# Attention's output projection as seven block products, four more weight blocks split by VectorE, and a longer lead for DMAs

## The chip, the cores and the metric

The kernel runs on one core of one Trainium2 chip. The metric is device time in microseconds (us), the median of several executions. Engines are named as the profile names them: PE (TensorE, matmuls), DVE (VectorE), ACT (ScalarE), POOL (GpSimd), SP (SyncE, which here only issues transfers). A transfer is a DMA. The profile lists one execution.

## The reference

Two layers of a streaming encoder on 512 tokens of width 1024, in float32. Layer 0 is a convolution module and an MLP, layer 1 is latent attention and an MLP; each part is normed before and after and added to the stream h.

```python
# layer 0, convolution module
u = h @ w_pw1 + b_pw1
a, gate = jnp.split(u, 2, axis=-1)
u = a * jax.nn.sigmoid(gate)
u = lax.conv_general_dilated(u, ...)  # 31 taps, one filter for each channel
u = jax.nn.silu(layer_norm(u, ln_g, ln_b))
return u @ w_pw2 + b_pw2
# MLP of both layers
return jnp.square(jax.nn.relu(h @ w1)) @ w2
# layer 1, attention: o holds the 8 heads' outputs, 512 x 1024
return o @ w_o
```

## The kernel before

**Precision.** Each float32 matrix is kept as two parts, hi (the value rounded to the matmul's format) and lo (what that leaves out). A product is three matmuls: hi x hi, hi x lo, lo x hi. A weight block is 128 x 1024, read by SP into `raw` (5 buffers); ACT's copy makes `wh` (5 buffers), and DVE's subtraction `wl` (6 buffers). `weight` does this, in the order of the table `USE`. For blocks chosen by `lo_by_dma` the lower part is made in another way: ACT writes -hi into `wl`, and POOL issues a transfer that reads the block from DRAM a second time and adds it to `wl` (an accumulating transfer). In the first pointwise product this holds for the blocks from the fifth on (`i >= 4`).

**Convolution module.** `w_pw1` is 16 blocks, taken in pairs (a and gate of 128 channels): "block 0" to "block 7" below are these pairs. After a pair, DVE scales both by the norm, ACT takes the sigmoid, DVE makes u. In blocks 0, 1 and 3 the 31 taps are run by DVE and ACT. In blocks 2, 4, 5, 6 and 7 they are run by PE with Toeplitz matrices (read from `cw` by SP, nine transfers for a block), and u goes to DRAM and back to be dealt out over the partitions: one transfer `dealt<-big` and four `uu<-dealt`, all issued by ACT (`deal_tokens`, then `taps_tensor`). The taps of block 2 stand on PE behind the pair of block 4. The vector table `vt` holds the biases that the sigmoid needs.

**MLP.** The second product is done by Strassen's scheme: the 2 x 2 blocks of each side (halves of tokens by halves of the inner dimension, halves of the inner dimension by halves of the columns) give seven products instead of eight. Sides that are sums or differences are made first: on the left by DVE, on the right by a POOL transfer that adds the second block to `raw` (sum) or by a second read and a DVE subtraction (difference). The results are added to or taken from the output blocks by DVE.

**Attention's output projection.** `wo` runs `by_tokens`: for the first half of the columns all four token blocks together, then for the second half one token block after the other. 8 weight blocks, 192 matmuls of 128 x 512. `post_norm` takes each finished block: ACT's square into `junk` (a sum for the norm), DVE's product with the gain (`big<-big,row`), and when a pair of token blocks (0 and 1, or 2 and 3) is complete, its norm (small `stat` operations) and four additions to h (`h<-big,stat,h`). Then `prenorm`: PE transposes h into `bc` (eight 128-blocks by two token blocks), ACT and DVE write hi and lo of the next input, and FF1 of layer 1 begins on it, on 256 tokens at a time at first. This passage is called the joint below.

**What sets the order.** The code above records operations; the planner (`schedule`) orders them by estimated costs, and the engines' instructions come out in that order, all with the line of `issue` (L640). Each engine runs its list in order. A transfer isn't issued more than `LEAD` (16000 ns) ahead of its due time. Where the planner expects PE to wait long for a new accumulator, it puts identity matmuls there (`mm<-ident`, `bc<-ident` without a second source).

Of the kernel before, what the change touches and what calls it, by code (L numbers as in the profile page):

```python
# [11 lines left out]
ALU = mybir.AluOpType  # L12
# [68 lines left out]
PRODUCTS = ((3, 6, 2, 1, 4, 5, 7),) * 2 + ((3, 1, 4, 5, 7), (3, 5, 1, 4, 7))  # L81


BLK = {}
USE = []
_cols, _names = [], []
# [27 lines left out]
def _out(*name):  # L114

    for dh in range(2):
        for ku in range(4):
            _blk(name + (dh, ku))
# [24 lines left out]
_blk(("kr",))  # L143
for _m in range(3):
    _blk(("dq", _m))
for _u in range(-1, 16):
    for _key in PROJECTIONS.get(_u, ()):
        _blk(_key, {"uv": 512, "uqr": 384, "uq": 384, "uk": 256}[_key[0]])
_out("wo")
_ff(1)  # L150
NBLK = len(_cols)

# [95 lines left out]

PORT = ("tensor_tensor", "scalar_tensor_tensor")

LEAD = 16000.0

BESIDE = 3000.0

# [389 lines left out]
def trunk(ctx: ExitStack, tc: tile.TileContext, xT, xN, wts, vec, along, rope, cw, out):  # L644
# [28 lines left out]
    def pair():  # L673
        return big(F32R), big(F32R)

    def tmp():
        return nc.tile(TMP)
# [53 lines left out]
    def weight(key):  # L731

        while key not in blocks:
            name, parts = USE[len(blocks)]
            i, n = BLK[parts[0][0]], _cols[BLK[parts[0][0]]]
            if name[0] in GAINS:
                blocks[name] = scaled(name, wts[i])
                continue
            raw, hi, lo = nc.tile(RAW), nc.tile(WH, F32R), nc.tile(WL, F32R)
            step = 256 if i < 2 else n  # L740
            for o in range(0, n, step):
                nc.sync.dma_start(out=raw[:, o : o + step], in_=wts[i, :, o : o + step])
            for other, sign in parts[1:]:
                if sign > 0:
                    nc.gpsimd.dma_start(out=raw, in_=wts[BLK[other]], accum_op=ALU.add)
                else:
                    second = nc.tile(RAW)
                    nc.sync.dma_start(out=second, in_=wts[BLK[other]])
                    for o in range(0, n, 512):
                        nc.vector.tensor_tensor(  # L750
                            out=raw[:, o : o + 512], in0=raw[:, o : o + 512], in1=second[:, o : o + 512], op=ALU.subtract
                        )
            src = raw if len(parts) > 1 else wts[i]
            if i >= 4 and lo_by_dma(name):
# [203 lines left out]
        return y  # L958


    def feed_forward(layer, X, F):


# [4 lines left out]
        for q in range(4):  # L968
# [5 lines left out]
            for m, (t0, n) in order:  # L974
# [4 lines left out]
                for th, (a, w) in enumerate((HA, HB)):  # L979
                    if t0 <= a < t0 + n:  # L980
# [4 lines left out]
            def terms(p):  # L985

                left, A = STRASSEN[p][0], []
                for u in range(2):
                    src = Z[left[0][0]][u]
                    if len(left) > 1:  # L990
                        d = tmp()
                        nc.vector.tensor_tensor(out=d, in0=src, in1=Z[left[1][0]][u], op=ALU.subtract)
                        src = d
                    A.append(pair())
                    split(src, slice(0, T), A[u])
                return A

            def sides(q, p):
                return [weight(("ff2", layer, q, p, u)) for u in range(2)]

            def product(pts, A, w, steps, first=True, last=True):

                for u, i in steps:
                    if i not in pts:
                        pts[i] = nc.tile(MM)
                    hi, lo = w[u]
                    for j in range(2):
                        cs, ts = slice(j * DH, (j + 1) * DH), slice(j * 2 * P + i * P, j * 2 * P + (i + 1) * P)
                        for k, (a, c) in enumerate(((A[u][0], hi), (A[u][0], lo), (A[u][1], hi))):
                            nc.tensor.matmul(  # L1010
                                pts[i], lhsT=a[:, ts], rhs=c[:, cs],
                                start=(first and u == 0 and j == 0 and k == 0), stop=(last and u == 1 and j == 1 and k == 2),
                            )
                return pts

            def collect(p, pts):
                for i, pt in pts.items():
# [12 lines left out]
                F[b][to[1]] = acc[quad[to]][i]  # L1030
                return b, to[1]

            steps = [(u, i) for u in range(2) for i in range(2)]
            for p in PRODUCTS[q]:
                A = terms(p)
                collect(p, product({}, A, sides(q, p), steps))
                if q == 3 and p in (5, 7):
                    for i in range(2):
                        yield done((0, int(p == 5)), i)
            if q > 1:  # L1040
                for p in TOGETHER:
                    both[q, p] = terms(p)
            if q == 3:

                pts = {p: product({}, both[2, p], sides(2, p), steps, last=False) for p in TOGETHER}
# [241 lines left out]
    def token_blocks():  # L1287
        return [[big() for _ in range(2)] for _ in range(TB)]

    def mixer_out(layer, gen):  # L1290

        MF, r2 = token_blocks(), one(f"r2_{layer}", [P, TB])
# [148 lines left out]

    for b in range(TB):
        nc.sync.dma_start(out=h[b], in_=order[b * P : (b + 1) * P])
    O = [pair() for _ in range(KT)]
    ALL = slice(0, T)
    V, QR, KN, QN, PN = {}, {}, {}, {}, {}

# [89 lines left out]

    def project(u):
        for kind, n in PROJECTIONS.get(u, ()):
            {"uqr": rotary, "uv": values, "uk": keys, "uq": queries}[kind](n)  # L1540

    project(-1)
# [16 lines left out]
    Xn, r2 = mixer_out(1, wo)  # L1559
    F = [[None, None] for _ in range(TB)]  # L1560

    def finish(bs, rho):
# [133 lines left out]
```

## Time and profile before

| | us |
|---|---|
| median of 3 runs | 1066.44 (1065.2 to 1067.63) |
| the profiled execution | 1068.46 |
| its span | 1066.7 |
| TensorE busy | 1045.5 (98%) |
| VectorE busy | 764.1 (72%) |
| ScalarE busy | 640.9 (60%) |

The mean granted TensorE clock of the profiled execution is 0.993 of full speed. In lines of the profile, `out<-in` names the tiles, `xN` counts instructions, and what stands in brackets at an end is the idle time before the instruction and what ended it. Busy times of neighbours on PE overlap, so a matmul's price is read from the distance of starts, or from a full window by its count. In windows the columns are length, busy time and count for each engine, granted clock, share of time that the 16 DMA engines were busy, and GB/s.

### The profile page before, as it was taken

The numbers are of one execution on the slowest core, as the hardware profiler recorded it, in microseconds if no ns is written. First come the engines' busy times: TensorE is split into PE (matmuls) and PEld (weight loads), VectorE is DVE, ScalarE is ACT, GpSimd is POOL, SyncE is SP. The second block draws the span as 40 slices with busy tenths as digits, with TensorE's granted clock in tenths as the row PEclk, the third lists the DMA queues.
The fourth block names the chain that finished last, engine by engine and source line by source line (L and its number), as shares of the span: only waits on it lengthen the run. The fifth ranks groups of instructions, "written<-read, shape, count | busy, mean of one in ns | idle before, by whom it ended". The sixth has DMA issues, their size and how long they took to land. (4 is left out here: it accounts for less than half of the span.)

```text
span 1066.7 us, 15181 instructions
## 1 busy us (share of the span) xinstructions
PE 1045.5 (98%) x5284; PEld 884.7 (83%) x5284; DVE 764.1 (72%) x1559; ACT 640.9 (60%) x1343; POOL 141.6 (13%) x165
## 2 busy tenths in 40 slices
PE   8989999999999999999999999999999999999996
PEld 7878988988888888888888888889888888888885
DVE  6497994857438737959988987547574495497698
ACT  8543497766545446545767877558565554454652
POOL 1110011100100100001104533301010010000010
PEclk9989999999999999999999999999999999999998
DMA  9995888657866848658923132557599388485684
GB/s 288 300 254 171 287 211 236 156 168 207 253 171 190 257 126 241 189 182 227 237 69 93 56 100 81 174 182 179 161 245 253 112 235 257 143 243 168 187 237 129
DMA packets 67613, 204.08 MB, mean 191 GB/s; under 512 B 7632, under 2 KB 13904, under 8 KB 67536
## 3 DMA queue, kind: packets, MB, share of 16 engines
q1 hardware_dynamic: 49680, 150.15, 40.9%
q0 software_dynamic: 13536, 49.29, 25.6%
q10 hardware_dynamic: 4320, 3.68, 1.1%
q8 instruction: 41, 0.67, 0.3%
q14 instruction: 36, 0.29, 0.1%
HBM read 197.58 MB, written 5.51 MB: 190 GB/s over the span
## 5 line engine op out<-in xcount | busy, mean ns | idle before, releaser
L640 PE MATMUL mm<-big,wh 128*128 128x512 f32 (+1 forms) x1512 | 441.1, 374 | 1.2 <-ACT wh L640 1.2
L640 PE MATMUL mm<-wh,big 128*128 128x512 f32 (+1 forms) x1216 | 374.7, 387 | 0.0
L640 ACT ACTIVATE wh<-raw 128x512 fp32r<-128x512 f32 (+2 forms) x444 | 251.0, 612 | 117.7 <-PE mm L640 73.8
L640 PEld LDWEIGHTS mm<-big,wh 128*128 128x128 f32 x1512 | 275.6, 188 | 52.4 <-ACT wh L640 1.5
L640 DVE TENSOR_TENSOR wl<-raw,wh 128x512 fp32r<-128x512 f32 (+1 forms) x356 | 227.7, 680 | 106.5 <-ACT wh L640 104.1
L640 PE MATMUL mm<-big,wl 128*128 128x512 f32 (+1 forms) x756 | 282.5, 374 | 0.0
L640 PEld LDWEIGHTS mm<-wh,big 128*128 128x128 f32 x1216 | 226.3, 188 | 46.9
L640 PE MATMUL mm<-wl,big 128*128 128x512 f32 (+1 forms) x608 | 234.9, 387 | 0.1
L640 PEld LDWEIGHTS mm<-big,wl 128*128 128x128 f32 x756 | 142.6, 189 | 25.7 <-DVE wl L640 0.5
L640 PEld LDWEIGHTS mm<-wl,big 128*128 128x128 f32 x608 | 114.2, 188 | 23.4 <-DVE wl L640 0.2
L640 POOL DMA_DIRECT2D raw<-wts x64 | 55.5, 867 | 572.7 <-DMA raw<-wts 190.4
L640 ACT ACTIVATE big<-tmp 128x256 f32<-128x256 f32 (+1 forms) x208 | 95.9, 493 | 43.2 <-DVE tmp L640 37.3
L640 DVE TENSOR_TENSOR big<-big,big 128x512 f32<-128x512 f32 (+4 forms) x103 | 69.8, 698 | 55.9 <-ACT big L640 55.6
L640 ACT ACTIVATE tmp<-mm 128x512 f32<-128x512 f32 (+1 forms) x75 | 41.7, 556 | 103.1 <-PE mm L640 102.0
L640 PE MATMUL mm<-big,big 128*128 128x256 f32 (+3 forms) x520 | 83.5, 310 | 1.8 <-DVE big L640 1.8
L640 PEld LDWEIGHTS mm<-big,big 128*128 128x128 f32 x520 | 73.1, 189 | 7.0 <-DVE big L640 2.3
L640 ACT ACTIVATE big<-mm 128x512 f32<-128x512 f32 (+5 forms) x106 | 56.6, 537 | 33.9 <-PE mm L640 32.9
L640 DVE TENSOR_TENSOR big<-tmp,big 128x512 fp32r<-128x512 f32 (+1 forms) x96 | 60.9, 642 | 15.3 <-ACT big L640 12.7
L640 DVE SCALAR_TENSOR_TENSOR big<-big,vt,big 128x512 fp32r<-128x512 f32 (+29 forms) x95 | 63.3, 736 | 8.0 <-ACT big L640 8.0
L640 DVE TENSOR_TENSOR big<-big,mm 128x512 f32<-128x512 f32 x96 | 63.7, 683 | 3.2 <-PE mm L640 2.8
L640 DVE TENSOR_TENSOR tmp<-big,big 128x512 f32<-128x512 f32 x80 | 53.3, 686 | 8.9 <-ACT big L640 8.9
L640 POOL DMA_DIRECT2D wl<-wts x30 | 26.1, 869 | 213.0 <-ACT wl L640 113.3
(90 smaller groups left out, 775.9 us busy)
## 6 DMA issues: line engine op xcount, KB each, us to landing
raw<-wts SPq DMA_DIRECT2D x222, 512.0 KB, 5.0
raw<-wts POOLq DMA_DIRECT2D x64, 512.0 KB, 7.9
wl<-wts POOLq DMA_DIRECT2D x30, 512.0 KB, 8.4
big<-cw SPq DMA_DIRECT2D x45, 256.0 KB, 5.6
big<-wts SPq DMA_DIRECT2D x12, 256.0 KB, 4.3
row<-along SPq DMA_DIRECT2D x5, 512.0 KB, 5.5
raw<-wts SPq DMA_DIRECT2D x12, 192.0 KB, 2.7
big<-xT SPq DMA_DIRECT2D x8, 256.0 KB, 4.2
```

Of the source, the lines that this page charges most:

```text
L640: return f(*args, **kwargs)
```

## The change

Three things change.

1. The output projection is done by the Strassen scheme that the MLP has. Attention's outputs go into eight blocks `Z` (two ACT copies of 256 columns for each head) in place of the eight pairs `O`; `terms` makes the left sides, `product` runs 24 matmuls of 128 x 512, `collect_wo` brings the results together (first write by ACT, the others by DVE). Product 3 is done during attention (unit 13 of 16), then 6, 4, 1, 5, 7, and last product 2 by token halves. Its right sides cost eight more reads on SP and eight accumulating transfers on POOL.
2. The blocks of the first pointwise product whose lower parts are made by accumulating transfers now begin at the ninth (`i >= 8`); those of the fifth to the eighth are made by DVE.
3. `LEAD` is 24000.

```diff
+WO_AT = {13: 3}
+WO_ORDER, LATE = (3, 6, 4, 1, 5, 7), (2,)
...
-LEAD = 16000.0
+LEAD = 24000.0
...
-            if i >= 4 and lo_by_dma(name):
+            if i >= 8 and lo_by_dma(name):
...
-        split(po, ALL, O[hd])
+        for th, (t0, n) in enumerate((HA, HB)):
+            j = hd % 2
+            nc.scalar.activation(Z[th, hd // 4][hd % 4 // 2][:, j * n : (j + 1) * n], po[:, t0 : t0 + n], AF.Copy)
...
+    def collect_wo(p, pts):
+        for i, pt in pts.items():
+            for (th, dh), sign in STRASSEN[p][2].items():
+                c = MF[2 * th + i][dh]
+                if (th, dh, i) not in made:
+                    made.add((th, dh, i))
+                    nc.scalar.activation(c, pt, AF.Copy, scale=float(sign))
+                else:
+                    nc.vector.tensor_tensor(out=c, in0=c, in1=pt, op=ALU.add if sign > 0 else ALU.subtract)
...
+            if 2 * hd + half in WO_AT:
+                product_wo(WO_AT[2 * hd + half])
...
-        for b, dh, pt in by_tokens(("wo",), O):
-            nc.scalar.activation(MF[b][dh], pt, AF.Copy)
-            yield b, dh
+        for p in WO_ORDER[EARLY:]:
+            product_wo(p)
+            for i in range(2):
+                for th, dh in STRASSEN[p][2]:
+                    if final[th, dh] == p:
+                        yield 2 * th + i, dh
+        A, w = ({p: f(p) for p in LATE} for f in (lambda p: terms(Z, p), lambda p: [weight(("wo", "", p, u)) for u in range(2)]))
+        for i in range(2):
+            for p in LATE:
+                collect_wo(p, product({}, A[p], w[p], [(0, i), (1, i)]))
+                for th, dh in STRASSEN[p][2]:
+                    if final[th, dh] == p:
+                        yield 2 * th + i, dh
```

`terms` and `product` are the functions that `feed_forward` had inside, moved out. All lists below are in program order, and a number behind a name tells tiles apart.

The order moves in three places. The first is the start of the program. POOL's transfers for lower parts, before (wl4 is the lower part of the fifth block):

```order
L640 DMA wl4_279<-wts 128x1024
L640 DMA wl5_311<-wts 128x1024
L640 DMA wl6_331<-wts 128x1024
L640 DMA wl7_356<-wts 128x1024
L640 DMA wl8_424<-wts 128x1024
L640 DMA wl9_453<-wts 128x1024
```

and after:

```order
L659 DMA wl8_367<-wts 128x1024
L659 DMA wl9_412<-wts 128x1024
L659 DMA wl10_496<-wts 128x1024
L659 DMA wl11_532<-wts 128x1024
L659 DMA wl12_633<-wts 128x1024
```

The first four are gone; their work stands on DVE as eight subtractions. On ACT, around the round trip of block 2 (`dealt0` and `uu00`; big44 is u of block 2), before:

```order
L640 DMA dealt0_529<-big44_518 128x512
L640 ACTIVATE wl10_532<-raw10_484 128x512 x2
L640 ACTIVATE wh10_547<-raw10_484 128x512 x2
L640 ACTIVATE big42_122<-big40_508,vt0_94 128x511
L640 ACTIVATE wl11_586<-raw11_544 128x512 x2
L640 ACTIVATE wh11_598<-raw11_544 128x512
L640 DMA uu00_109<-dealt0_529 32x4x128 x4
```

and after:

```order
L659 ACTIVATE wl10_496<-raw10_444 128x512 x2
L659 ACTIVATE wh10_523<-raw10_444 128x512
L659 ACTIVATE wl11_532<-raw11_486 128x512 x2
L659 ACTIVATE tmp13_542<-tmp12_529,vt0_94 128x512
L659 ACTIVATE wh10_523<-raw10_444 128x512
L659 DMA dealt0_565<-big44_559 128x512
L659 ACTIVATE wh11_577<-raw11_486 128x512 x2
L659 DMA uu00_109<-dealt0_565 32x4x128 x4
```

The splits of the eleventh block (raw10) now stand ahead of `dealt0`. The buffer of raw10 is the one that the sixteenth block's read (raw15) needs, so that read is now released just ahead of `dealt0`, and not behind it.

The second is DVE at the joint, where the first pair's norm ends (h00 and h10 are token blocks 0 and 1; mm225 and mm226 the accumulators of product 2). Before:

```order
L640 TENSOR_TENSOR stat46_7224<-stat46_7224 128x2 x2
L640 TENSOR_TENSOR big541_7341<-big541_7341,row3_6873 128x512
L640 SCALAR_TENSOR_TENSOR stat46_7224<-stat46_7224 128x2 x2
L640 TENSOR_TENSOR stat46_7224<-stat46_7224 128x2
L640 SCALAR_TENSOR_TENSOR stat46_7224<-stat46_7224 128x2 x2
L640 SCALAR_TENSOR_TENSOR h00_1443<-big538_7219,stat46_7224,h00_1443 128x512
L640 SCALAR_TENSOR_TENSOR h10_1450<-big540_7229,stat46_7224,h10_1450 128x512
```

and after:

```order
L659 SCALAR_TENSOR_TENSOR stat46_7456<-stat46_7456 128x2 x2
L659 TENSOR_TENSOR big390_7313<-big390_7313,mm225_7461 128x512
L659 TENSOR_TENSOR stat46_7456<-stat46_7456 128x2
L659 TENSOR_TENSOR big391_7089<-big391_7089,mm225_7461 128x512
L659 SCALAR_TENSOR_TENSOR stat46_7456<-stat46_7456 128x2 x2
L659 TENSOR_TENSOR big392_7332<-big392_7332,mm226_7506 128x512
L659 SCALAR_TENSOR_TENSOR h00_1247<-big386_7307,stat46_7456,h00_1247 128x512
L659 SCALAR_TENSOR_TENSOR h10_1249<-big388_7326,stat46_7456,h10_1249 128x512
```

The h rows now stand behind a subtraction that reads mm226, the last accumulator of the projection.

The third is PE at the same joint, where the first transposes (`bc<-ident,h`) stand. Before:

```order
L640 MATMUL mm219_7339<-wl143_7291,big390_7061 128x512
L640 MATMUL mm219_7339<-wh143_7208,big392_7131 128x512
L640 MATMUL bc55_7378<-ident0_105,h00_1443 128x128
L640 MATMUL bc56_7380<-ident0_105,h00_1443 128x128
L640 MATMUL mm219_7339<-wl143_7291,big392_7131 128x512
L640 MATMUL mm219_7339<-wh143_7208,big391_7070 128x512
L640 MATMUL bc55_7378<-ident0_105,h10_1450 128x128
```

and after:

```order
L659 MATMUL mm226_7506<-wl149_7431,big580_7364 128x512
L659 MATMUL mm226_7506<-wh149_7421,big581_7408 128x512
L659 MATMUL bc55_7547<-ident0_105 128x128 x7
L659 MATMUL bc55_7547<-ident0_105,h00_1247 128x128
L659 MATMUL bc56_7556<-ident0_105,h00_1247 128x128
L659 MATMUL bc55_7547<-ident0_105,h10_1249 128x128
```

Before, the transposes stand among the projection's matmuls; after, behind them, with seven identity matmuls between. Two more stand a little later, ahead of an FF1 accumulator (mm227), and three more than before ahead of the last taps, those of block 7. The whole program has 24 matmuls of the projection fewer and 12 identity matmuls more.

More of the change, by code (lines that the diff above doesn't have):

```diff
@@ L81 @@
 PRODUCTS = ((3, 6, 2, 1, 4, 5, 7),) * 2 + ((3, 1, 4, 5, 7), (3, 5, 1, 4, 7))
+WO_AT = {13: 3}
+WO_ORDER, LATE = (3, 6, 4, 1, 5, 7), (2,)
+EARLY = len(WO_AT)
 BLK = {}
@@ L145, with _strassen @@
     _blk(("dq", _m))
+def _strassen(of, name):
+    p, u = name[-2:]
+    return name, tuple((of + (dh, 2 * kh + u), sign) for (kh, dh), sign in STRASSEN[p][1])
 for _u in range(-1, 16):
+    if _u in WO_AT:
+        for _v in range(2):
+            USE.append(_strassen(("wo",), ("wo", "", WO_AT[_u], _v)))
     for _key in PROJECTIONS.get(_u, ()):
@@ L149 @@
 _out("wo")
+USE = [u for u in USE if u[0][0] != "wo" or len(u[0]) > 3]
+for _p in WO_ORDER[EARLY:] + LATE:
+    for _u in range(2):
+        USE.append(_strassen(("wo",), ("wo", "", _p, _u)))
 _ff(1)
@@ L958, in prenorm, with terms, product @@
         return y
+    def terms(Z, p):
+        left, A = STRASSEN[p][0], []
+        for u in range(2):
+            src = Z[left[0][0]][u]
+            if len(left) > 1:
+                d = tmp()
+                nc.vector.tensor_tensor(out=d, in0=src, in1=Z[left[1][0]][u], op=ALU.subtract)
+                src = d
+            A.append(pair())
+            split(src, slice(0, T), A[u])
+        return A
+    STEPS = [(u, i) for u in range(2) for i in range(2)]
+    def product(pts, A, w, steps, first=True, last=True):
+        for u, i in steps:
+            if i not in pts:
+                pts[i] = nc.tile(MM)
+            hi, lo = w[u]
+            for j in range(2):
+                cs, ts = slice(j * DH, (j + 1) * DH), slice(j * 2 * P + i * P, j * 2 * P + (i + 1) * P)
+                for k, (a, c) in enumerate(((A[u][0], hi), (A[u][0], lo), (A[u][1], hi))):
+                    nc.tensor.matmul(
+                        pts[i], lhsT=a[:, ts], rhs=c[:, cs],
+                        start=(first and u == 0 and j == 0 and k == 0), stop=(last and u == 1 and j == 1 and k == 2),
+                    )
+        return pts
     def feed_forward(layer, X, F):
@@ L984, in feed_forward @@
                         )
[L985 to L996, printed above, removed]
             def sides(q, p):
                 return [weight(("ff2", layer, q, p, u)) for u in range(2)]
[L1001 to L1014, printed above, removed]
             def collect(p, pts):
@@ L1031, in done @@
                 return b, to[1]
-            steps = [(u, i) for u in range(2) for i in range(2)]
             for p in PRODUCTS[q]:
-                A = terms(p)
-                collect(p, product({}, A, sides(q, p), steps))
+                A = terms(Z, p)
+                collect(p, product({}, A, sides(q, p), STEPS))
                 if q == 3 and p in (5, 7):
@@ L1041, in feed_forward @@
                 for p in TOGETHER:
-                    both[q, p] = terms(p)
+                    both[q, p] = terms(Z, p)
             if q == 3:
-                pts = {p: product({}, both[2, p], sides(2, p), steps, last=False) for p in TOGETHER}
+                pts = {p: product({}, both[2, p], sides(2, p), STEPS, last=False) for p in TOGETHER}
                 w = {p: sides(3, p) for p in TOGETHER}
@@ L1288, in token_blocks, with mixer_out @@
         return [[big() for _ in range(2)] for _ in range(TB)]
-    def mixer_out(layer, gen):
-        MF, r2 = token_blocks(), one(f"r2_{layer}", [P, TB])
+    def mixer_out(layer, gen, MF=None):
+        MF, r2 = MF or token_blocks(), one(f"r2_{layer}", [P, TB])
         Xn = [pair() for _ in range(KT)]
@@ L1443, in trunk @@
         nc.sync.dma_start(out=h[b], in_=order[b * P : (b + 1) * P])
-    O = [pair() for _ in range(KT)]
+    Z = {(th, kh): [big() for _ in range(2)] for kh in range(2) for th in range(2)}
+    MF = token_blocks()
     ALL = slice(0, T)
@@ L1540, in project, with product_wo @@
             {"uqr": rotary, "uv": values, "uk": keys, "uq": queries}[kind](n)
+    made = set()
+    def collect_wo(p, pts):
[7 more added lines that the diff above has]
+                    nc.vector.tensor_tensor(out=c, in0=c, in1=pt, op=ALU.add if sign > 0 else ALU.subtract)
+    def product_wo(p, steps=STEPS):
+        collect_wo(p, product({}, terms(Z, p), [weight(("wo", "", p, u)) for u in range(2)], steps))
     project(-1)
@@ L1554, in wo @@
     def wo(MF):
-        for b, dh, pt in by_tokens(("wo",), O):
-            nc.scalar.activation(MF[b][dh], pt, AF.Copy)
-            yield b, dh
-    Xn, r2 = mixer_out(1, wo)
+        order = WO_ORDER + LATE
+        final = {to: [p for p in order if to in STRASSEN[p][2]][-1] for to in ((0, 0), (0, 1), (1, 0), (1, 1))}
+        for p in WO_ORDER[EARLY:]:
[11 more added lines that the diff above has]
+                        yield 2 * th + i, dh
+    Xn, r2 = mixer_out(1, wo, MF)
     F = [[None, None] for _ in range(TB)]
```

## The prediction

> **What bounds the kernel now.** I read the busy shares first, then what TensorE waited for, then windows around its waits, then the queues there. The page's head:
>
> ```profile
> span 1066.7 us, 15181 instructions
> PE 1045.5 (98%) x5284; PEld 884.7 (83%) x5284; DVE 764.1 (72%) x1559; ACT 640.9 (60%) x1343; POOL 141.6 (13%) x165
> ```
>
> TensorE is busy 98% of the span, so time moves in two ways only: matmuls go, or its waits and slow stretches do. Its waits, longest groups first (us in total, times, longest):
>
> ```profile
> PE mm L640 <- DMA uu<-dealt: 3.7, 1, 3.7
> PE mm L640 <- DVE big L640: 1.8, 3, 0.7
> ```
>
> The first is the one wait worth an edit: the first TensorE taps (block 2) need the tokens that go through DRAM and back (dealt, uu). Windows (length, busy per engine, then granted clock, DMA share):
>
> ```profile
> core 0: us, PE busy (x) PEld busy (x) DVE busy (x) ACT busy (x) POOL busy (x), PEclk, DMA share, GB/s
> 63.40:67.30 3.90, 0.21 (x2) 0.04 (x1) 3.90 (x7) 3.90 (x8) 0.95 (x2) 0.87 0.77 237
> 67.30:70.50 3.20, 3.20 (x15) 3.20 (x16) 3.20 (x6) 2.73 (x6) 1.64 (x2) 0.50 0.89 182
> 70.50:74.00 3.50, 3.50 (x22) 3.50 (x22) 3.50 (x7) 0.00 (x0) 0.00 (x0) 0.63 1.05 245
> 482.00:520.00 38.00, 38.00 (x171) 30.96 (x170) 36.34 (x68) 25.20 (x53) 9.51 (x13) 1.00 0.94 249
> 711.70:724.50 12.80, 12.80 (x65) 10.62 (x64) 8.79 (x23) 9.40 (x24) 1.60 (x2) 1.00 0.50 149
> 771.34:809.80 38.46, 38.46 (x169) 31.55 (x168) 25.90 (x43) 26.76 (x51) 3.44 (x4) 1.00 0.91 259
> ```
>
> TensorE stands for 3.69 us, and then runs at half clock for 3.2 us and partly for 3.5 more. The last row prices a matmul of 512 columns at full clock: 38.46 / 168 = 0.229 us. The row at 711 is the present joint between the output projection and FF1: TensorE has no idle time there. The row at 482 is a stretch of FF2, which is Strassen already: TensorE full with VectorE at 36.3 of 38 us, so a stretch so loaded can be carried.
>
> **The change, part by part.**
>
> *Matmuls.* 7 products of 24 replace 192: 24 x 0.229 = **-5.5 us**, certain.
>
> *Weights and sums of the projection.* 8 more reads on SP, 8 accumulations on POOL, VectorE's additions: the kinds of work that FF2 has at full rate (482 row), so I take 0, with TensorE as cover. If a weight is late, FF1's first blocks are, which is the second rival.
>
> *Product 3 among the attention heads.* It gives 24 matmuls to a stretch where TensorE waits for VectorE (window 560 to 711, same columns). It can fill at most those waits; I take **-0.6**, between 0 and -0.9, since one place fills the one or two nearest.
>
> ```profile
> PE mm L640 <- DVE big L640: 1.0, 2, 0.7
> PE bc L640 <- DVE big L640: 0.8, 2, 0.6
> ```
>
> *The joint.* Before, blocks 2 and 3 of the second half of the columns were left when the first half's norm began, 48 matmuls (11 us) beside the chain below. Now only product 2 is left, and VectorE's list puts its last subtraction ahead of the four h rows: that chain starts when TensorE is out of projection work. Its steps, from the trace (start, length):
>
> ```profile
> 715.55 2.74 DVE L640 SCALAR_TENSOR_TENSOR h<-big,stat,h 128x512 f32<-128x512 f32 x4
> ...
> 723.64 0.88 DVE L640 SCALAR_TENSOR_TENSOR big<-bc,vt,big 128x256 fp32r<-128x256 f32 x2 [0.65 <-ACT big L640]
> 716.39 0.63 ACT L640 ACTIVATE junk<-h 128x512 f32<-128x512 f32 x1 [3.12 <-issue]
> ...
> 717.78 0.84 ACT L640 ACTIVATE big<-bc,vt 128x256 fp32r<-128x256 f32 x2
> ...
> 723.82 1.20 ACT L640 ACTIVATE wh<-raw 128x512 fp32r<-128x512 f32 x2
> 716.57 0.38 PE L640 MATMUL bc<-ident,h 128*128 128x128 f32 x2
> ...
> 717.25 0.82 PE L640 MATMUL bc<-ident,h 128*128 128x128 f32 x6
> ...
> 151.55 1.50 PE L640 MATMUL mm<-ident 128*128 128x128 f32 x12
> 152.96 0.53 PE L640 MATMUL mm<-wh,big 128*128 128x512 f32 x1
> L640 DVE TENSOR_TENSOR big<-big,mm 128x512 f32<-128x512 f32 x96 | 63.7, 683 | 3.2 <-PE mm L640 2.8
> ```
>
> From TensorE's last projection matmul: subtraction 0.68 plus 0.2 to start, then 716.57 - 715.55 = 1.02 to the first transposes: 1.9. The second h row 0.4 (717.25 less 716.57 and two transposes). The first pair of splits: 717.78 - 717.25 = 0.5, then hi 0.84 and lo 0.88 half overlapped, 1.4; 0.8 of it is transposes that are work in any case: 1.1. Then two waits that ACT's list shows, one split behind two weight halves (0.6 each, 1.20 for two: 0.9 net), one behind a square (0.63). The second half's first h row, 0.4. Together 1.9 + 0.4 + 1.1 + 0.9 + 0.6 + 0.4 = **+5.3**. The planner fills part with nine identity matmuls (six take 1.41 us from 151.55 to 152.96, so 0.23 each), inside the 5.3. Low end 2.1, these nine alone; high end 8.0, no FF1 matmul before the last split: 724.52 - 715.55 + 0.9, less 16 transposes at 0.11.
>
> *Three more identity matmuls at the last taps:* 3 x 0.23 = **+0.7**, since TensorE doesn't wait there now.
>
> *The DRAM round trip.* First the traffic from 15 to 50 (share of the accumulating queue; KB and us to landing of reads) and SP's waits for landings, then the queues and VectorE in time:
>
> ```profile
> q0 software_dynamic: 864, 3.15, 47.4%
> raw<-wts SPq DMA_DIRECT2D x9, 512.0 KB, 9.1
> big<-cw SPq DMA_DIRECT2D x9, 256.0 KB, 15.2
> vt<-vec SPq DMA_DIRECT2D x1, 178.5 KB, 12.2
> ...
> SPq L640 <- DMA big<-cw: 14.0, 7, 7.9
> 24.70 0.48 SPq L640 DMA_DIRECT2D vt<-vec  x1
> ...
> 46.59 5.58 SPq L640 DMA_DIRECT2D raw<-wts  x4
> ...
> 49.18 0.33 ACTq L640 DMA_DIRECT2D dealt<-big  x1
> 55.99 6.52 ACTq L640 DMA_DIRECT2D uu<-dealt  x4
> 62.55 0.63 ACT L640 ACTIVATE wh<-raw 128x512 fp32r<-128x512 f32 x1 [8.56 <-DMA raw<-wts]
> 38.02 1.15 DVE L640 SCALAR_TENSOR_TENSOR big<-tmp,vt,tmp 128x512 f32<-128x512 f32 x1 [6.01 <-ACT tmp L640]
> 43.04 1.71 DVE L640 SCALAR_TENSOR_TENSOR big<-tmp,vt,tmp 128x512 f32<-128x512 f32 x2
> ```
>
> In this program the transfers of SP and ACT use eight completion counters in turn, and a transfer's issue waits until the one eight places earlier has landed (SP's 14.0 us for its own loads). The four uu transfers are therefore not issued together: 6.5 us apart, the last held by a weight read (the [8.56 <-DMA raw<-wts]). That is the last of the four raw reads that SP issued up to 52.2, and it took about 10 us in a full DMA system. The last uu lands 67.30 - 62.2 = 5.1 later. So the wait is traffic, not VectorE: block 2's u was done at 44.75.
>
> The change takes four of six accumulations out of 15 to 50 (47.4% of 35 us = 16.6 us of all engines; 4/6 is 11 us), so the Toeplitz loads, which SP issues one landing at a time, end some 8 us earlier, and three of the four raws with them. The price is on VectorE: eight lower parts, and by its new list 16 instructions between u of block 0 and u of block 2 (11.7 us at 0.61 to 0.66 each and 1.1 for the wide ones). With u of block 0 at 34 instead of 38 (its sigmoid needs vt, which landed at 24.7 + 12.2 = 36.9 in the crowd), u of block 2 comes at 34 + 11.7 = 45.7, about as now. Dealt 46 to 53, uu issued by 55, landed by 60: before TensorE arrives at 63.6. I take the wait, **-3.7**, and what the half clock cost: 13 matmuls at 0.43 (3.20 us for about 7.5 pitches) instead of 0.23, 13 x 0.2, **-2.7**. Ends: 0, nothing gained, and -6.4; the nearest row is the traffic one, so I take the full gain. The lead of 24 us for transfers moves reads earlier, bounded by five raw buffers: 0.
>
> [...] The halving came with a stand of 3.69 us, and stands of 0.7 us (the second wait) left the clock alone. [...]
>
> **Sum:** -5.5 - 0.6 + 5.3 + 0.7 - 3.7 - 2.7 = -6.5. The profiled execution took 1068.46, so 1062.0; it stands 2.0 above the median 1066.44 (runs 1065.2 to 1067.63). From the median 1059.9. I put 1060.5, because the profiled stand may be longer than the usual one. The likeliest case alone: 1058.5 to 1062.5.
>
> **The rivals.** (1) *The round trip's wait stays*, held by something else in the freed traffic: only -5.5 - 0.6 + 5.3 + 0.7 = -0.1, so 1066.3. For it: the DMA share is 0.9 to 1.0 through the stage and the longer lead offers more reads. Against: SP's reads are bounded by buffers.
> (2) *The joint is dearer*: 8.0 instead of 5.3, and a stand in one piece that halves the clock as at 67 (6.7 us at half, 3.4 more if it comes whole): 1063 to 1066.5, middle 1064. For it: weight halves ahead of splits on ACT; against: identity matmuls break the stand.
> (3) *Slower*: in the new order the fourth uu's predecessor is no longer a weight read but a Toeplitz load, the second that SP issues after the last raw, itself released by ACT just ahead of dealt. Priced at 15.2 us (the load's row) from dealt's issue, and 5.1 more: with u of block 0 at 38.0 as now, dealt at 49.7, uu at 70.0, 2.7 later than now: -0.1 + 2.7 = 1069.0. It decides when dealt is issued after 47.0, and is a measurable loss from 49. Against: the 15.2 was measured in the crowded stretch.
> (4) *The joint is hidden too*: only the nine identity matmuls, 2.1: 1057.3. Against: VectorE's list.
>
> **Chances.** As forecast 0.52; (1) 0.16; (2) 0.13; (3) 0.10; (4) 0.09. About 0.2% (2.1 us) is what this measurement tells from no change. Faster: 0.52 + 0.09 + 0.10 of (2) = 0.71; same: 0.03 of (2) and 0.14 of (1) = 0.17; slower: (3) and 0.02 of (1), 0.12. The range, 1057 to 1067, leaves out (3), a third of (1) and a third of (4), 0.18.
>
> **What the profile after would show.** Right: no wait on uu<-dealt over 0.7 us and a clock of 1.0 between 63 and 75; wl reads gone before 30 us, vt landed before 34; at the joint, 4 to 6 us of identity matmuls and idle time between the last projection matmul and steady FF1. Wrong: ACT held by a Toeplitz load ahead of uu; a granted clock under 1 after the projection; TensorE waiting for wh or wl of the projection, which I put at 0.

## The result and the profile after

The changed kernel takes 1088.71 us (median of 4 runs, 1088.19 to 1090.97) against 1065.82; ratio 1.0223, 95% interval 1.0205 to 1.0242. It is slower by about 23 us, where about 6 us faster was forecast. The head of its page, and what TensorE waited for:

```profile
span 1087.1 us, 15316 instructions
PE 1050.5 (97%) x5284; PEld 886.1 (82%) x5284; DVE 810.1 (75%) x1607; ACT 653.4 (60%) x1369; POOL 156.7 (14%) x177
```

```profile
PE mm L659 <- DMA uu<-dealt: 8.5, 1, 8.5
PE bc L659 <- DVE big L659: 7.5, 8, 3.4
PE mm L659 <- DVE wl L659: 4.5, 4, 2.1
```

TensorE's busy time rose by 5.0 us, although 24 matmuls went: busy time counts the stretches at half clock too (2.95 of the 3.00 us from 139.20, at a clock of 0.51). The waits moved. The round trip's wait is still the longest, but it is another round trip: not the first, of block 2, but the last, of block 7. And VectorE, which cost TensorE 1.8 and 1.5 us before in its two largest groups, costs 7.5 and 4.5.

Windows of the changed kernel: the wait before the last taps, the half clock behind it, then attention's last part with the projection, and the joint (length, busy per engine, granted clock, DMA share):

```profile
core 0: us, PE busy (x) PEld busy (x) DVE busy (x) ACT busy (x) POOL busy (x), PEclk, DMA share, GB/s
130.50:139.20 8.70, 0.24 (x3) 0.05 (x1) 3.57 (x9) 2.08 (x5) 0.00 (x0) 0.78 1.04 334
139.20:142.20 3.00, 2.95 (x14) 2.98 (x15) 0.00 (x0) 0.00 (x0) 0.00 (x0) 0.51 0.83 328
...
640.00:737.00 97.00, 86.67 (x428) 72.95 (x428) 84.74 (x173) 65.33 (x145) 39.41 (x34) 0.95 0.76 210
737.00:746.00 9.00, 7.20 (x54) 6.11 (x53) 8.53 (x20) 8.90 (x24) 0.86 (x1) 1.00 1.04 246
```

The kernel before, profiled a second time (run e14 below), has this in the stretch from 640 us to its joint:

```profile
640.00:711.00 71.00, 70.14 (x374) 59.38 (x373) 40.98 (x118) 44.19 (x100) 18.97 (x16) 1.00 0.50 155
```

VectorE there works 41 us of 71, and 84.7 of 97 after; TensorE idles 0.9 us before and 10.3 after, with a granted clock of 0.95: in three places, each behind a wait of 1.6 to 3.4 us, it runs at half clock for 3.4 us (from 664.4, 681.5 and 698.5).

Where the 25 us between the two spans (1087.1 and 1062.2, e14) came in is read by when the same matmul starts in both traces (called "by matmuls" below). (The kernel before's own two profiles, compared so, differ by 5.7 us at the first round trip and by at most 1.2 us more behind it.) The result: 0.6 gained up to the last taps; 10.8 lost there, of which 2.7 come back just behind, where the kernel before has small waits of its own; 1.1 lost slowly through layer 0's MLP, so 8.6 behind near 500 us; 23.8 behind when FF1 of layer 1 runs steadily; 24.9 at the end. So two places make nearly all of it: the last taps, and the 200 us of attention, projection and joint, which lose 15.2 although 5.5 of matmuls went there.

### The profile page after: what moved, and what is told of

It reads as the page before. It is cut to its first block, busy times and chain, and to the rows that moved or that the text cites. A ratio compares the mean times of both kernels' runs of the same rounds, so it can differ in the third digit from the quotient of the medians.

```text
span 1087.1 us, 15316 instructions
## 1 busy us (share of the span) xinstructions
PE 1050.5 (97%) x5284; PEld 886.1 (82%) x5284; DVE 810.1 (75%) x1607; ACT 653.4 (60%) x1369; POOL 156.7 (14%) x177
## 4 chain that ended last, share of the span: by engine, by line
PE 83%; DVE 10%; ACT 3%; DMA 2%; issue 1%; ACTq 0%; DVEq 0%
PE mm L659 81%; DVE big L659 7%; ACT big L659 2%; PE bc L659 2%; DMA uu<-dealt 1%; DVE stat L659 1%; DVE wl L659 1%; DVE tmp L659 0%; ACT junk L659 0%; ACT wl L659 0%; ACT wh L659 0%; DVE raw L659 0%; DMA vt<-vec 0%; DVE h L659 0%; ACTq L659 0%
## 5 line engine op out<-in xcount | busy, mean ns | idle before, releaser
L659 ACT ACTIVATE wh<-raw 128x512 fp32r<-128x512 f32 (+2 forms) x456 | 259.6, 613 | 205.6 <-PE mm L659 164.6
L659 DVE TENSOR_TENSOR wl<-raw,wh 128x512 fp32r<-128x512 f32 (+1 forms) x366 | 239.8, 692 | 171.1 <-ACT wh L659 166.5
L659 POOL DMA_DIRECT2D raw<-wts x72 | 62.2, 869 | 586.6 <-DVE wl L659 198.2
L659 ACT ACTIVATE big<-tmp 128x256 f32<-128x256 f32 (+1 forms) x218 | 102.9, 499 | 49.1 <-DVE tmp L659 47.3
L659 DVE TENSOR_TENSOR big<-big,big 128x512 f32<-128x512 f32 (+4 forms) x108 | 73.1, 695 | 12.2 <-ACT big L659 11.6
L659 DVE TENSOR_TENSOR big<-tmp,big 128x512 fp32r<-128x512 f32 (+1 forms) x106 | 72.6, 693 | 8.2 <-ACT big L659 5.9
L659 DVE TENSOR_TENSOR big<-big,mm 128x512 f32<-128x512 f32 x112 | 73.4, 678 | 2.0 <-PE mm L659 1.8
L659 DVE TENSOR_TENSOR tmp<-big,big 128x512 f32<-128x512 f32 x90 | 61.0, 691 | 1.1 <-ACT big L659 1.1
L659 POOL TENSOR_TENSOR wl<-raw,wh 128x512 fp32r<-128x512 f32 (+2 forms) x38 | 45.7, 1264 | 80.6 <-ACT wh L659 46.6
```

What stands on the lines that cost most here:

```text
L659: return f(*args, **kwargs)
```

## The experiments

Every run was timed beside the kernel before, on one chip per batch. The first four take the change apart.

**e1: the lead back at 16 us.**

```diff
-LEAD = 24000.0
+LEAD = 16000.0
```

> The changed kernel with the lead for transfers put back to 16 us. Theory L (the longer lead sends accumulating reads of the second pointwise product's weights ahead of the last DRAM round trip): the 8.5 us wait before the last taps and the 2.7 us of half clock behind it go, so 1089 - 11 = about 1078. Rival P (TensorE merely arrives 6 us earlier there, because of the pointwise edit): the wait stays, about 1088.

1080.83 us, ratio 1.0158 (1.0131 to 1.0185). 8 us came back. The wait for the last round trip is 3.4 us instead of 8.5, with 3.4 us at half clock behind it. So the lead does much of it, but not all.

**e2: only the pointwise edit, on the kernel before.**

```diff
-            if i >= 4 and lo_by_dma(name):
+            if i >= 8 and lo_by_dma(name):
```

> The kernel before with only the four pointwise blocks' lower parts on VectorE. Forecast's step for the first round trip: the 3.7 us wait and 2.7 us of half clock go, no new wait: about 1060. Rival P: the wait turns up again before the last taps: 1066 or more.

1066.84 us, ratio 1.0017 (1.0007 to 1.0027): no gain. Its profile has no wait for either round trip. Against e14's trace it gains 1.0 us at the first round trip, which is about all that e14 has to give there; it loses 1.4 in the first 30 us, and 2.9 behind 560 us, where the edit does nothing itself.

**e3: only the lead of 24 us, on the kernel before.** The edit is that of e1 the other way round.

> The kernel before with only the lead at 24 us. Theory L: a wait of 5 to 9 us on the last round trip, with half clock behind it, while the first wait stays: 1073 to 1078. Rival P: no change, 1066.

1068.72 us, ratio 1.0032 (1.0015 to 1.0049), with a wide scatter, 1066.4 to 1074.6: less than theory L's 1073 to 1078 in the median. The profiled execution is the slowest of the ten, at 1074.6, and has the waits that theory L foretold, 2.4 us on the first round trip and 5.0 on the last:

```profile
PE mm L640 <- DMA uu<-dealt: 7.4, 2, 5.0
```

The first accumulating read of the second pointwise product is issued at 124.37 in it, ahead of the last four `uu` (from 128.18); in e14 it comes behind them (129.41 and 125.49).

**e4: only the projection by Strassen** (lead 16 us and `i >= 4` in the changed kernel).

> The kernel before with only the output projection by Strassen (lead 16 us, pointwise blocks as before). Theory G (POOL's subtractions for the projection's lower parts stretch VectorE's instructions, and TensorE waits for these): +12 to +16 with waits on VectorE between attention and the projection, 1078 to 1082. Rival (it is the longer lead that crowds POOL and VectorE there): only the joint's 5.3 less the 5.5 saved, 1066.

1076.70 us, ratio 1.0107 (1.0084 to 1.0129). Strassen alone costs 11 us, although it takes 5.5 us of matmuls away; that is just under theory G's range and far from the rival's 1066. The three parts alone add up to 15.7 (11.2 + 3.2 + 1.3); together they cost 23, so some 7 us are from their meeting. Lead and round trip are part of that: with the lead at 16 us, Strassen and the pointwise edit together wait 3.4 us there (e1), each alone not at all.

The second batch works on the whole changed kernel.

**e5: the projection's lower parts by VectorE alone.**

```diff
-ATT = ("uq", "uqr", "uk", "uv", "wo")
+ATT = ("uq", "uqr", "uk", "uv")
```

> The changed kernel, with the lower parts of the projection's weights made by VectorE alone (POOL keeps those of the other attention weights). Theory G: of the 15.8 us by which VectorE's instructions are stretched beside POOL's subtractions between 640 and 740 us most go, against 14 more subtractions of 0.68 (9.5 us) on VectorE; TensorE waits 5 to 10 us less: 1079 to 1084. Rival H (VectorE simply has too much work there, whoever helps): no gain or a loss, 1089 to 1094.

1079.52 us, ratio 1.0125 (1.0099 to 1.0152): 9 us better than the changed kernel, though VectorE now makes 29 subtractions for weights in this part where it made 12. TensorE's waits from 640 us to the end of the projection fall from 10.4 us to 2.2, and the half clock there is gone. By matmuls, the changed kernel loses 14.6 us against e14 between 640 us and steady FF1 (735 us in e14), and e5 gains 0.1. (The profiled execution of e5, its slowest, loses 6 us near 1058, at a wait of 2.9 us with 6.8 us at half clock; so the whole gain is smaller.) Rival H falls: VectorE has more to do and TensorE waits less. How that can be stands in the groups of VectorE, changed kernel, 640 to 740 us (busy us, mean ns of one):

```profile
L659 DVE TENSOR_SCALAR big<-big,stat 128x128 f32<-128x128 f32 (+3 forms) x16 | 12.7, 806 | 0.3
L659 DVE TENSOR_TENSOR big<-tmp,big 128x512 fp32r<-128x512 f32 x10 | 12.1, 1215 | 0.3 <-ACT big L659 0.3
L659 DVE TENSOR_TENSOR wl<-raw,wh 128x512 fp32r<-128x512 f32 x12 | 11.6, 988 | 0.0
L659 DVE TENSOR_TENSOR big<-big,mm 128x512 f32<-128x512 f32 x15 | 9.9, 677 | 0.5 <-PE mm L659 0.4
...
L659 DVE TENSOR_TENSOR raw<-raw,raw 128x512 f32<-128x512 f32 x4 | 4.9, 1228 | 0.0
```

and in e5, 640 to 728 us:

```profile
L659 DVE TENSOR_TENSOR wl<-raw,wh 128x512 fp32r<-128x512 f32 x29 | 19.8, 701 | 1.3 <-ACT wh L659 1.2
L659 DVE TENSOR_TENSOR big<-big,mm 128x512 f32<-128x512 f32 x15 | 9.8, 680 | 0.0
...
L659 DVE TENSOR_SCALAR big<-big,stat 128x128 f32<-128x128 f32 (+3 forms) x16 | 7.4, 471 | 0.1
L659 DVE TENSOR_TENSOR big<-tmp,big 128x512 fp32r<-128x512 f32 x10 | 6.8, 684 | 0.0
L659 DVE TENSOR_TENSOR raw<-raw,raw 128x512 f32<-128x512 f32 x4 | 2.6, 681 | 0.0
```

The same instructions are longer in the changed kernel: 806 ns against 471, 1215 against 684, 1228 against 681. The group that reads an accumulator (`big<-big,mm`) isn't: 677 and 680. What stands beside the long ones is POOL's subtraction of weights. One instruction of VectorE undisturbed, and the same kind at the worst place:

```profile
656.47 0.35 DVE L659 TENSOR_SCALAR big<-big,stat 128x256 f32<-128x256 f32 x1
...
671.56 0.17 DVE L659 RECIPROCAL stat<-stat 128x1 f32<-128x1 f32 x1 [0.43 <-ACT big L659]
671.76 4.87 DVE L659 TENSOR_SCALAR big<-big,stat 128x256 f32<-128x256 f32 x1
676.56 0.68 DVE L659 TENSOR_TENSOR big<-mm,big 128x512 fp32r<-128x512 f32 x1
```

and POOL:

```profile
669.65 1.30 POOL L659 TENSOR_TENSOR wl<-raw,wh 128x512 fp32r<-128x512 f32 x1 [6.96 <-ACT wh L659]
670.88 1.78 POOL L659 DMA_DIRECT2D raw<-wts  x2
672.03 4.45 POOL L659 TENSOR_TENSOR wl<-raw,wh 128x512 fp32r<-128x512 f32 x3
```

A VectorE instruction of 0.35 us takes 4.87: it ends at 676.63, just behind POOL's third subtraction in a row (672.03 to 676.48). TensorE's longest wait on VectorE, 3.4 us until 680.99, comes right behind it. Instructions that read an accumulator aren't stretched so: after 540 us, 36 of VectorE's overlap POOL's tensor instructions by over 0.3 us, and the longest takes 0.69.

**e6: product 3 after attention.**

```diff
-WO_AT = {13: 3}
+WO_AT = {}
```

> The changed kernel with product 3 done after attention instead of within it. Rival E (the early product crowds the attention heads): the waits between 640 and 700 us go, 1080 or less. Theory G: POOL's subtractions still stand beside VectorE, so 1086 to 1091.

1087.34 us, ratio 1.0208 (1.0190 to 1.0226): nothing that can be told from the changed kernel. Rival E falls.

**e7: products 6 and 2 last.**

```diff
-WO_ORDER, LATE = (3, 6, 4, 1, 5, 7), (2,)
+WO_ORDER, LATE = (3, 4, 1, 5, 7), (6, 2)
```

> The changed kernel with the order 3, 4, 1, 5, 7 and then 6 and 2 together by token halves, so that the first half of the tokens is complete 48 matmuls (11 us) before the end. Forecast's term for the joint: 5 us come back, 1083 to 1084. Rival (the joint is held by VectorE's backlog, whatever stands last): 1087 to 1090.

1081.85 us, ratio 1.0155 (1.0140 to 1.0170): 7 us better. But not by the joint alone: VectorE's stretch between 640 us and the joint fell as well, and so did the half clock there (table at e13). The joint itself isn't shorter: the first transposes still stand behind the last projection matmul (730.06 after 729.82), and identity matmuls and idle time behind it make 4.0 us, as in the changed kernel. So the 7 us don't price the joint.

**e8: accumulating transfers with a lead of 16 us, others 24.**

```diff
+                lead = 16000.0 if "accum_op" in o.kwargs else LEAD
-                if way[1] == "dma_start" and o.rank > now + LEAD:
+                if way[1] == "dma_start" and o.rank > now + lead:
```

> The changed kernel with the lead of 24 us for plain transfers and 16 us again for accumulating ones. Theory L: the three accumulating reads that stand ahead of the last round trip go behind it, and the 8.5 us wait with its half clock shrinks to 3 us or less: 1081 to 1083. Rival (it is SP's plain reads that crowd it): the wait stays, 1087 to 1090.

1087.49 us, ratio 1.0193 (1.0167 to 1.0218), and the wait is 8.8 us. It doesn't decide: the trace has accumulating reads at 119.0, 120.6 and 121.6 us, still ahead of the last four `uu` (127.1). Not their own lead holds them but their turn behind ACT's copies, which end POOL's waits.

So e9 takes three of the four accumulating reads away that stand ahead of or beside the last round trip. In the changed kernel POOL's and ACT's queues before the last taps are (the first of the four reads, at 112.66, has landed by 122.5):

```profile
119.21 0.86 POOL L659 DMA_DIRECT2D wl<-wts  x1 [5.68 <-ACT wl L659]
120.25 0.86 POOL L659 DMA_DIRECT2D wl<-wts  x1 [0.17 <-issue]
124.41 0.86 POOL L659 DMA_DIRECT2D wl<-wts  x1 [3.29 <-ACT wl L659]
...
116.86 0.34 ACTq L659 DMA_DIRECT2D dealt<-big  x1
123.87 1.85 ACTq L659 DMA_DIRECT2D uu<-dealt  x4
```

and the traffic from 114 to 139 us:

```profile
DMA  9999999999999999999999999999999999999999
q1 hardware_dynamic: 1481, 5.30, 55.5%
q0 software_dynamic: 576, 2.10, 42.1%
...
uu<-dealt ACTq DMA_DIRECT2D x4, 64.0 KB, 12.2
```

The four small transfers take 12.2 us in the median, and the accumulating queue takes 42% of all engines meanwhile. In the kernel before, the first such read is issued after the four have landed, and they take 2.7:

```profile
129.90 2.21 ACTq L640 DMA_DIRECT2D uu<-dealt  x4
...
134.12 0.86 POOL L640 DMA_DIRECT2D wl<-wts  x1 [50.23 <-PE mm L640]
```

**e9: the first three blocks of the second pointwise product by VectorE.**

```diff
-    return name[0] in ("pw1", "pw2")
+    return name[0] == "pw1" or (name[0] == "pw2" and (name[1] or name[2] == 3))
```

> The changed kernel with the first three blocks of the second pointwise product's weights split by VectorE, so that no accumulating read is issued before the last round trip has landed. Theory L, narrowed (it is these accumulating reads that delay the round trip, whatever brings them forward): the 8.5 us wait and its half clock go, about 1078. Rival (SP's plain reads alone crowd it): a wait of 5 us or more stays, 1085 to 1089.

1080.78 us, ratio 1.0139 (1.0115 to 1.0162): 8 us better. No wait for a round trip is left, and the window from 120 to 140 us has TensorE busy for 19.85 of 20 at full clock, with the DMA engines at 0.95. The edit doesn't do quite what its expectation says, for one accumulating read, that of the fourth block, is still issued ahead of the four:

```profile
121.45 0.86 POOL L659 DMA_DIRECT2D wl<-wts  x1 [52.00 <-ACT wl L659]
...
125.55 2.01 ACTq L659 DMA_DIRECT2D uu<-dealt  x4
```

They take 5.3 us in the median. Over all profiles the last four `uu` take 1.9 to 3.2 us with no accumulating read under way (before, e2, e4, e10, e14), 3.3 to 5.4 with one (e9, e11, e12, e15), and 6.1 to 14.1 with two or three under way within 2 us of the first `uu` (the other eight). The engines are nearly full in e9 too, mostly with plain reads (64.5% against 18.7% for the accumulating queue, 120 to 135 us), and there is no wait; theory L holds in its narrowed form.

**e10: e4 with the projection's lower parts by VectorE alone** (the edit of e5).

> Only the projection by Strassen (lead 16 us, pointwise blocks as before), its lower parts made by VectorE alone. Theory G: of the 11.2 us that Strassen alone costs, 7 to 9 go: 1068 to 1070, the rest being the joint. Rival H: 1076 or more.

1068.09 us, ratio 1.0027 (1.0012 to 1.0043). Of the 11 us that Strassen alone costs, 8.6 are gone without POOL's subtractions. By matmuls in the two profiles, 6.9 of it is between 640 us and FF1; about 2 is the first round trip, where e4's execution stood for 2.09 us and ran at half clock for 3.4, and e10's stood for 1.52 without that, so this part may be chance. What is left is about 3 us above the kernel before.

**e11 and e12: e5, e7 and e9 together, with a lead of 16 and of 24 us.**

> All three repairs on the changed kernel: lead 16 us, projection's lower parts by VectorE, products 6 and 2 last by token halves, first three blocks of the second pointwise product by VectorE. If theories G, L and the joint's cover hold together: Strassen's 5.5 and some of the first round trip's wait are gained, 1058 to 1063. Rival (VectorE is now full and hands its load on as waits): 1066 to 1072.

> The same three repairs with the lead left at 24 us. If the lead does harm only through the accumulating reads ahead of the round trip: within 2 us of the kernel with 16 us. If it does more: 4 us or more above it.

1075.56 us, ratio 1.0092 (1.0071 to 1.0114), and 1069.49, ratio 1.0034 (1.0020 to 1.0047). Neither expectation was met: e11 is above its rival's range too, and the longer lead is better by 6 us. No wait for a round trip is left in either, and VectorE's stretch from 640 us to the joint is 1.7 us in both, yet neither beats the kernel before. In e11 about 6 us are lost against e14 between 508 and 559 us, at the start of attention, where it has waits of up to 1.0 us and 3.4 us at half clock; e12 loses less than 1 there. Each edit moves the plan elsewhere too, so the gains of the repairs don't add up.

**e13: all of the projection's lower parts on POOL.**

```diff
-                engines = VG if name[0] in ATT else ("vector",)
+                engines = ("gpsimd",) if name[0] == "wo" else VG if name[0] in ATT else ("vector",)
```

> The changed kernel with all 28 subtractions for the projection's lower parts on POOL (about half of them there in the changed kernel). Theory G: each costs VectorE about 1.1 us of stretch, so the 15.8 us between 640 and 740 us become 25 to 30; VectorE is spared 9.5; 1090 to 1096. Rival H (VectorE has too much work): it is relieved of 9.5 us and TensorE waits less, 1080 to 1085.

1088.20 us, ratio 1.0224 (1.0207 to 1.0241), the same as the changed kernel. Neither expectation was met in time. By matmuls, though, it loses 8.7 us between 640 us and FF1 where the changed kernel loses 14.6, and 3 more than that kernel ahead of 640 us, 2 of them at the last taps. Two stretches of half clock fewer make 3.4 of that difference; VectorE's load, ten subtractions less, may make the rest, although the stretch grew. That the load alone isn't the cause is shown by e5, where VectorE has seventeen more. In the table, "stretch" is what VectorE's instructions take beyond the shortest of their kind and shape in the same profile, where that is over 0.3 us, from 640 us to the joint (counted so, the 15.8 of two expectations is 18.5); "half clock" is TensorE's time at it from 640 us to FF1, and "lost" is the time lost there against e14, by matmuls, net of the 5.5 us that the change saves:

| kernel | POOL's weight subtractions | stretch, us | half clock, us | lost, us |
|---|---|---|---|---|
| before (e14) | 10 | 1.4 | 0 | 0 |
| e5 | 3 | 2.3 | 0 | -0.1 |
| e10 | 2 | 2.5 | 0 | -1.1 |
| e4 | 18 | 8.0 | 0 | 5.8 |
| e1 | 13 | 9.5 | 3.4 | 4.2 |
| e7 | 21 | 12.8 | 0 | 5.9 |
| changed | 20 | 18.5 | 10.2 | 14.6 |
| e13 | 31 | 21.8 | 3.4 | 8.7 |

It isn't the number alone: the ten of the kernel before stand beside 1.4 us of stretch. There, of VectorE's instructions that overlap one of POOL's subtractions by over 0.2 us, 13 read an accumulator and 5 don't; in the changed kernel it is 11 and 17. So 5 meetings with an instruction that reads only the buffer memory stand beside 1.4 us of stretch, and 17 beside 18.5. The longest single one, 4.87 us for 0.35, has three of POOL's in a row beside it.

**e14: the kernel before, profiled again** (no edit; one execution).

> The kernel before, profiled once more. Theory W: the first round trip's wait varies from one execution to the next, and the profile the forecast was made from had a long one (mean clock 0.993, where the timed runs show 0.995 to 0.998); here 1 to 2.5 us with at most one stretch of 3.4 us at half clock, 1063 to 1066. Rival: 3.7 us and 6.8 us at half clock again, 1067 to 1069.

1063.99 us. Its span is 1062.2, and TensorE stands for 0.75 us until 64.49, not for 3.69, and just under theory W's 1 to 2.5. The window over the same place:

```profile
63.00:73.00 10.00, 9.25 (x78) 8.78 (x77) 10.00 (x16) 6.37 (x15) 1.91 (x3) 1.00 0.98 240
```

The granted clock is 1.00 throughout. The 6.4 us that the forecast took for a property of the kernel belonged to one execution: the two profiles differ by 5.7 us at this place and by little elsewhere. The other profiles with the old pointwise edit (e3, e4, e10, e15) stand there for 2.35, 2.09, 1.52 and 1.38 us, and the first two run at half clock for 3.4. The timed executions of the kernel before have mean clocks of 0.994 to 0.998; the first profile had 0.993.

**e15: e10 with products 6 and 2 last.**

> Strassen with the projection's lower parts by VectorE (lead 16 us, pointwise blocks as before), and products 6 and 2 last by token halves. If the joint still costs the forecast's 5 us there, the cover brings 3 to 5 of it back: 1063 to 1065, at or under the kernel before. Rival (VectorE's backlog holds the first half's norm, whatever stands last on TensorE): 1067 to 1071.

1081.50 us, ratio 1.0159 (1.0144 to 1.0174). Neither expectation was met. Against e10's profile, 15 us are lost: about 3.5 at the last taps (a wait of 2.2 us on the round trip and 3.4 at half clock), 4 at the start of attention, 4 between 640 us and FF1, the rest in small pieces. The joint is to be seen here, for the first transposes stand among the projection's matmuls again (from 724.91, with the last projection matmul at 732.27). TensorE is still busy for only 16.03 of the 20.10 us from 724.90 on, and its three longest waits there end with ACT (1.2 and 0.95) and VectorE (1.6). So the missing cover alone isn't what the joint costs. Whether it would be cheaper in a plan held fixed elsewhere wasn't tried.

## Why the prediction was wrong, point by point

- **Matmuls, -5.5:** the count is right, and nothing in the runs speaks against the price; it is covered by what follows.
- **The first round trip, -6.4:** right as a mechanism, wrong in size. The steps came nearly as forecast: `dealt` was issued at 45.87 (46 was forecast), the fourth `uu` at 55.19, not held by the Toeplitz load, and the last landed at 60.02 (60). None of the eleven profiles with the new edit waits there; the six with the old one stand for 0.75 to 3.69 us. But e14 has 0.75 us and no half clock, and e2, which has this edit alone, gains nothing in all. The step that failed is the one that took a price from one profiled execution that stood 2.0 above the median and had a clock of 0.993; the text saw this, and corrected by half a microsecond.
- **The lead, 0:** failed. The forecast looked at SP's raw buffers only. The reads that came forward are accumulating ones on POOL, ahead of the last round trip: 8.5 us of wait and 6.8 us at half clock, 10.8 lost there against e14. e9 shows the cause. That the lead alone brings them forward is shown by e3; that with 16 us Strassen and the pointwise edit together still do so in part, by e1. The forecast followed the first round trip and none of the other four.
- **Weights and sums of the projection, 0:** failed, and it is the larger step: 14.6 us lost between 640 us and FF1. FF2 was taken as proof that VectorE can be this full. But in that stretch of FF2 POOL subtracts nothing; it issues transfers and clears memory, and VectorE makes most lower parts (kernel before, 482 to 520 us):

```profile
L640 POOL DMA_DIRECT2D raw<-wts x7 | 6.4, 908 | 22.8 <-DVE wl L640 13.2 <-DVE tmp L640 3.3 <-DMA raw<-wts 2.9
L640 POOL MEMSET big<- 64x512 f32 (+2 forms) x4 | 2.4, 590 | 0.1
L640 POOL DMA_DIRECT2D wl<-wts x2 | 1.7, 862 | 8.0 <-ACT wl L640 5.4 <-DMA raw<-wts 2.6
...
L640 DVE TENSOR_TENSOR wl<-raw,wh 128x512 fp32r<-128x512 f32 x20 | 13.2, 688 | 1.5 <-ACT wh L640 1.5
```

The projection's are shared with POOL, and beside POOL's subtractions an instruction of VectorE takes up to 14 times as long (4.87 us for 0.35). e5 and e10 show 9.2 and 8.6 us; with them goes the wait for the projection's lower parts (`DVE wl`, 4.2 us from 640 to 737 us), which the forecast named as a sign of being wrong. The profile before could have told it: between 542 and 640 us 15 instructions of VectorE are stretched there by 9.8 us in all, counted as in the table.
- **Product 3 within attention, -0.6:** not to be seen (e6).
- **The joint, +5.3:** near in size. In the changed kernel TensorE goes from the last projection matmul at 736.65 to 746 with nine identity matmuls (2.2 us) and 1.8 us of idle time, 4.0 in all; in e10 it is 2.8. That it is the missing cover which costs it was argued from VectorE's list and isn't shown, and e15, which has cover and still stands for 4.1 us, speaks against it as the only reason.
- **Three identity matmuls at the last taps, +0.7:** they stand within a wait of 8.5 us, so they cost nothing by themselves.
- **Rivals:** the third, slower by a round trip, had the right kind of mechanism at the wrong one of five round trips.

What stays open: e10, without POOL's subtractions, is still 3 us above the kernel before instead of 5.5 below it. By matmuls its profile gains only 1.1 us on e14 between 640 us and FF1, where 5.5 of matmuls went; the joint takes 2.8 of the difference. It loses 1.9 between 540 and 640 us and 1.5 behind FF1, which is close to what two profiles of one kernel differ by. VectorE's load (79.0 of 82 us from 640 to 722 us) may have a part in it, but no run separates these.

## What to carry to other kernels

Before an engine is given more work, look at what its neighbour does at the same time: on VectorE and POOL, count the instructions that read only the buffer memory, not their busy time. Here these were the stretched ones (up to 4.87 us for 0.35), and beside POOL's tensor instructions none that reads an accumulator took over 0.69. When transfers are moved forward, follow each later transfer that TensorE waits for, not only the one that the edit is about. And take the price of a wait from several executions: here the profile with a lower mean clock (0.993) than the timed runs (0.994 to 0.998) had a longest wait of 3.69 us, and at the same place the second profile (0.997) had 0.75.

## What was not expected of the hardware

A VectorE instruction of 0.35 us took 4.87 beside three POOL subtractions of 4.45 in a row, and none that reads an accumulator took longer than 0.69 beside POOL's tensor instructions. Four transfers of 64 KB took 12.2 us in the median with the accumulating queue at 42% of the DMA engines, 5.3 with one of that queue's reads under way and the engines nearly as full, and 1.9 to 3.2 with none. The clock was halved after shorter stands than the prediction's 3.69 us, and not always for the same time: 2.09 us in e4 brought 3.4 us at half clock, as 3.42 in e1 and 5.02 in e3 did, while 8.5 and 3.69 brought 6.8. The length of the stand alone doesn't decide: 1.63 us in the changed kernel (until 697.4) was followed by 3.4 at half clock, 2.04 in e9 (until 661.8) and 1.52 in e10 by none.
